# Three, not six, activation sums of the last feed-forward product kept in DRAM, and the sums of the first feed-forward matmul placed later in the program

## The chip, the cores and the metric

The kernel runs on one core of a Trainium2 chip. The metric is the device time of one execution in microseconds (us); lower is better. The engines of the core work from queues of their own and wait for each other through semaphores: PE (TensorE, matrix multiplication), ACT (ScalarE), DVE (VectorE), POOL (GpSimd) and SP (SyncE, which here only issues DMAs). An engine takes its instructions in the order of its program; an instruction that waits holds up those behind it.

## What is computed

One decoder layer on 1024 tokens of 1024 channels in float32: a pooling and attention mixer, a normalised residual, a feed-forward block, a second normalised residual, and a gated input at the end. The change lies in the feed-forward block and in what is prepared for the gate beside it:

```
h  = layer_norm(ALPHA * x + concat(pool, attn) @ w_out)      # 1024 x 1024
ff = square(relu(h @ w_ff1)) @ w_ff2                         # 1024 -> 4096 -> 1024
h  = layer_norm(ALPHA * h + ff)
gate = sigmoid(h @ w_ple_gate + b_ple_gate)                  # 1024 x 1024
out  = h + gate * (p @ w_ple)
```

## The kernel before, in words

**Number format.** Every matrix product is made of three PE passes (`mm3`, L115 to L117). Each operand is split into a high part, which ACT casts (`high`, L100), and a low part, which DVE gets by subtraction (`low`, L105); the passes are high by high, high by low and low by high. So before PE can multiply a fresh operand, ACT and then DVE must have been over it.

**Products in seven.** The feed-forward matmuls work on 2 x 2 blocks with seven block products in place of eight, so sums and differences of blocks are needed on the way. These are the DVE additions of `add` (L120).

**First feed-forward matmul.** The 4096 hidden channels are 16 pairs `p` of two 128-channel blocks; two pairs make a quad `q`. For each pair there are up to seven products, `a11, s2, s3, s1, a12, s4, a22` in this order (the first eight pairs did `a11` and `a12` earlier in the program). A product is 12 matmuls of 512 columns. The loop over `order` splits the weight operand of the product four places ahead (`AHEAD`), then multiplies the present one (`prod`), then calls `finish`, which forms the activation blocks. Split weights live in the six buffers of tag `ws` (`part`). When the second pair of a quad is done, the four blocks of activations are written to DRAM by POOL's queue (`f_dram`, L680). In this loop two extra pieces of work are placed:

- `hidden_sum(q)` (L700 on): one DVE addition of two activation blocks of the quad, in place (`v = v + ...`, 128 x 1024), and a DMA of the sum to `s_dram[q]` on POOL's queue (L702). It is wanted by the very last of the seven products of the second matmul, number 2, whose left operand is the sum of two blocks. It is done for six quads (`NQUAD - NKEEP`), each being queued in `late` and taken from it at a product `s3` of an even pair. Since it overwrites a block that is also being written to `f_dram`, it must wait until that write has ended.
- `weight_sums(k)`, for k = 0 to 3 at pairs 6 to 9: two DMAs bring rows of `w_gate` (L691, into two `ws` buffers), four DVE additions form sums of them, four DMAs put them into DRAM (`g_dram`, L697) for the gate matmul at the end. All of it stands behind product `s1` of the pair.

At the start of the last four pairs' products, four `pre` buffers of weights for the second matmul are fetched (L761), partly with a summing DMA on POOL's queue (L766).

**Second feed-forward matmul.** Seven products (`SEQUENCE` = 1, 5, 4, 3, 7, 6, 2) over eight quads each (`QORDER` = 6, 7, 0, 1, 2, 3, 4, 5) make 56 units. A unit is 24 matmuls. Quads 6 and 7 are still in SBUF; the others are read back once into `hidden` (six buffers of tag `c`) and stay there. While unit u is multiplied, `prepare(u + 1)` splits its operands, the activations into `w` (two buffers) and the weights into `right` (tile `x7`, shown as `x`). A left operand that is a sum is added on DVE into a `st` buffer (two of them); in product 2, for quads 0 to 5, `fetch_sum` instead loads it from `s_dram` into such a buffer by SP's queue (L776).

During product 2, SP's queue also carries the weights (L761), the write and the four reads of a transposition through DRAM for each normalised block (`flip`, L429 and L431), and the loads of the gate's weights (`gate_load`, L109). Each gate load needs a `ws` buffer and is split by ACT and DVE into a `c` buffer; `c` in the rows below is such a split gate weight, `w` and `x` are the two operands of the next unit.

A scheduler that simulates the program sets the final order on each engine, so instructions move by some places beyond what the code says.

Of the kernel before, what the change touches and what calls it, by code (L numbers as in the profile page):

```python
# [7 lines left out]
F32 = mybir.dt.float32  # L8
# [4 lines left out]
P = 128  # L13
D = 1024
S = 1024
HALF = 512
# [4 lines left out]
NQUAD = NPAIR // 2  # L21
# [27 lines left out]
NKEEP = 2  # L49
# [10 lines left out]
}  # L60
BLOCK = {"a11": 0, "a12": 1, "a21": 2, "a22": 3}
NPRE = 8
PLAIN = 4
HALVES = (slice(0, HALF), slice(HALF, D))
NLAST = NPAIR - 4
# [4 lines left out]
def layer(ctx, tc, xT, x, pT, w_in, w_pool, pscale, sinks, w_out, ln1, w1, w2, ln2, w_ple, w_gate, bgate, bias, rcount, out):  # L70
# [48 lines left out]
    def add(o, a, b, op=ALU.add):  # L119
        nc.vector.tensor_tensor(out=o, in0=a, in1=b, op=op)  # L120
# [14 lines left out]

    h_dram = [tc.dram_tile([P, D], F32, name=f"hd{n}") for n in range(NT)]
    t_dram = [tc.dram_tile([P, 4, 2 * P], F32, name=f"td{n}") for n in range(2 * NT)]
    s_dram = [tc.dram_tile([P, 2, HALF], F32, name=f"sd{q}") for q in range(NQUAD - NKEEP)]
    g_dram = {t: [tc.dram_tile([P, 2, HALF], F32, name=f"g{t}{i}") for i in range(2)] for t in ("T1", "T2", "T3", "T4")}
    f_dram = [tc.dram_tile([P, 2, 2, 2, HALF], F32, name=f"fd{q}") for q in range(NQUAD - NKEEP)]  # L140

# [531 lines left out]
    def hidden_block(p, m, n, make):  # L673
        key = (p // 2, m, n)
        if key not in FF:
            FF[key] = nat([P, 2, HALF])
        dst = FF[key][:, p % 2, :]
        make(dst)
        if p % 2 and p // 2 < NQUAD - NKEEP:
            nc.gpsimd.dma_start(out=f_dram[p // 2][:, m, n], in_=FF[key])  # L680
            if n == 1:
                made.append(key)
                if len(made) % 2 == 0:
                    late.append(lambda q=p // 2: hidden_sum(q))

    made, late, sums_a = [], [], {}

    def weight_sums(k):
        r = [part((P, 2, HALF), F32) for _ in range(2)]
        for i in range(2):  # L690
            nc.sync.dma_start(out=r[i], in_=w_gate[(4 * i + k) * P : (4 * i + k + 1) * P, :].rearrange("p (h c) -> p h c", h=2))  # L691
        add(r[0][:, 0], r[0][:, 1], r[0][:, 0], ALU.subtract)
        add(r[0][:, 1], r[1][:, 1], r[0][:, 1], ALU.subtract)
        add(r[1][:, 1], r[1][:, 1], r[0][:, 0], ALU.subtract)
        add(r[1][:, 0], r[1][:, 0], r[1][:, 1], ALU.subtract)
        for name, i, h in (("T1", 0, 0), ("T3", 0, 1), ("T2", 1, 1), ("T4", 1, 0)):
            nc.sync.dma_start(out=g_dram[name][k // 2][:, k % 2], in_=r[i][:, h])  # L697
# [73 lines left out]

    def fetch_sum(u):
        i, q = units[u]
        if i == 2 and q < NQUAD - NKEEP:
            sums_a[u] = stage([P, 2, HALF])
            nc.sync.dma_start(out=sums_a[u], in_=s_dram[q])  # L776

    ready = {}
    for i in range(len(order) + AHEAD):
        if i == order.index((NLAST, "a11")):  # L780
            begin = wide("pre", [P, 4, 2, HALF], F32)
            for u in range(4):
                fetch(u)
        if i < len(order):
            with tc.issue_after((diff[3][1] if i == AHEAD else lows[-1]).ins):
                ready[i] = w_split(source(*order[i]))
        if i < AHEAD:
            continue
        p, name = order[i - AHEAD]
        xb, where, more = STEPS[name]  # L790
        if not more:
            B[p, where] = bank()
        prod(B[p, where], ready.pop(i - AHEAD), xb, more)
        if late and p % 2 == 0 and name == "s3":
            late.pop(0)()
        if 6 <= p < 10 and name == "s1":
            weight_sums(p - 6)
        finish(p, name)
        if i - AHEAD < 4:
            with tc.issue_after(diff[3][1].ins):  # L800
                last_sum(i - AHEAD)
# [347 lines left out]
```

## Time and profile before

| what | us |
|---|---|
| runs shown | 985.11, 986.88, 988.04 |
| median of the runs shown | 986.88 |
| the profiled execution's own time | 986.92 |
| its span, first to last instruction | 985.1 |
| first feed-forward loop on PE, about | 320 to 569 |
| second feed-forward matmul on PE, about | 569 to 878 |
| product 2, its last eighth, about | 834 to 878 |

Times in the text count from the start of the span. In a timeline row, the first number is the start, the second the duration, then engine, source line, operation, written tile <- read tiles; in brackets is the idle time of the engine before the row and what ended it. A matmul row's duration is longer than the distance to the next start, because matmuls overlap; it is the distance of starts that tells whether PE is held up. In the chain of waits a row is start, duration, and what was done or waited for. "SPq" rows are the issue of a DMA by SP's queue.

### The profile page before, as it was taken

Reading aid. Unit: us, or ns where it says so; the run is one execution under the profiler, and the core shown is the slowest. Engines: PE = TensorE matmul, PEld = TensorE weight load, DVE = VectorE, ACT = ScalarE, POOL = GpSimd, SP = SyncE. Lnnn points to the kernel's source line nnn. Section 1 sums busy time; section 2 is a strip of 40 time slices with the busy share of each in tenths; the row PEclk is TensorE's granted clock in tenths of the full one; section 3 lists DMA queues with packets and bytes.
Section 4 is the critical chain, followed back from the end, with each engine's and each line's share of the span. In section 5 each row is a group of like instructions: output and inputs, shape, how many; then the busy total and the mean of one; then the engine's idle time right before and its main releaser. Section 6 shows DMA issues by size and latency. Waiting matters only on the chain.

```text
span 985.1 us, 12301 instructions
## 1 busy us (share of the span) xinstructions
PE 975.0 (99%) x4474; PEld 808.3 (82%) x4474; DVE 750.0 (76%) x1188; ACT 470.9 (48%) x749; POOL 110.0 (11%) x148
## 2 busy tenths in 40 slices
PE   9999999999999999999999999999999999999998
PEld 7888887888888888888888888888888888878887
DVE  5798888895869877667557766887647699599985
ACT  5676666543576434433444433433433344454341
POOL 0013552020010000111000000100011110001000
PEclk9999999999999999999999999999999999999999
DMA  6512142623162644897364793676798867962741
GB/s 220 182 65 86 44 150 86 203 92 112 65 214 86 211 153 149 305 297 264 114 258 172 291 319 137 157 249 193 196 225 186 227 158 231 287 200 92 240 150 54
DMA packets 52125, 175.28 MB, mean 178 GB/s; under 512 B 6112, under 2 KB 11360, under 8 KB 49248
## 3 DMA queue, kind: packets, MB, share of 16 engines
q1 hardware_dynamic: 41776, 140.02, 42.2%
q0 software_dynamic: 8704, 29.89, 12.2%
q10 hardware_dynamic: 1584, 4.59, 1.2%
q8 instruction: 35, 0.57, 0.2%
q14 instruction: 26, 0.21, 0.1%
HBM read 140.39 MB, written 34.08 MB: 177 GB/s over the span
## 4 chain that ended last, share of the span: by engine, by line
PE 84%; DVE 6%; DMA 5%; issue 3%; ACT 1%; POOL 0%; SPq 0%; DVEq 0%; ACTq 0%; POOLq 0%
PE f L117 18%; PE f L116 18%; PE f L115 18%; PE mm L115 8%; PE mm L116 8%; PE mm L117 8%; DMA ws<-in_w_gate 3%; DMA fd<-n 1%; PE pt L321 1%; DVE w L105 1%; PE s L298 1%; PE s L297 1%; DMA td<-n 1%; DVE x L105 1%; DVE st L120 1%
## 5 line engine op out<-in xcount | busy, mean ns | idle before, releaser
L116 PE MATMUL f<-x,w 128*128 128x512 f32 x448 | 174.3, 390 | 0.9 <-DVE x L105 0.9
L117 PE MATMUL f<-x,w 128*128 128x512 f32 x448 | 173.9, 389 | 0.0
L115 PE MATMUL f<-c,ws 128*128 128x512 f32 (+1 forms) x420 | 162.6, 387 | 0.0
L116 PE MATMUL f<-c,ws 128*128 128x512 f32 (+1 forms) x420 | 162.5, 387 | 0.0
L117 PE MATMUL f<-c,ws 128*128 128x512 f32 (+1 forms) x420 | 161.6, 388 | 0.5 <-DVE ws L105 0.5
L115 PE MATMUL f<-x,w 128*128 128x512 f32 x448 | 147.3, 390 | 0.9 <-ACT x L100 0.9
L100 ACT CAST w<-st 128x1024 fp32r<-128x1024 f32 (+2 forms) x66 | 65.6, 998 | 100.0 <-issue 58.0
L105 DVE TENSOR_TENSOR w<-st,w 128x1024 fp32r<-128x1024 f32 (+2 forms) x66 | 77.5, 1176 | 46.7 <-ACT w L100 46.5
L116 PEld LDWEIGHTS f<-x,w 128*128 128x128 f32 x448 | 84.1, 188 | 20.0 <-DVE x L105 2.6
L115 PEld LDWEIGHTS f<-x,w 128*128 128x128 f32 x448 | 83.9, 188 | 19.2 <-ACT x L100 1.8
L117 PEld LDWEIGHTS f<-x,w 128*128 128x128 f32 x448 | 84.1, 188 | 17.2
L117 PEld LDWEIGHTS f<-c,ws 128*128 128x128 f32 x420 | 78.8, 188 | 17.7 <-DVE ws L105 1.7
L116 PEld LDWEIGHTS f<-c,ws 128*128 128x128 f32 x420 | 78.9, 188 | 16.2
L115 PEld LDWEIGHTS f<-c,ws 128*128 128x128 f32 x420 | 78.9, 188 | 16.0
L105 DVE TENSOR_TENSOR x<-ws,x 128x1024 fp32r<-128x1024 f32 x54 | 65.7, 1217 | 0.1
L100 ACT CAST ws<-st 128x512 fp32r<-128x512 f32 x48 | 29.8, 621 | 65.7 <-DVE st L120 34.6
L100 ACT CAST x<-ws 128x1024 fp32r<-128x1024 f32 x54 | 56.6, 1049 | 5.2 <-PE f L117 3.5
L115 PE MATMUL mm<-c,w 128*128 128x512 f32 x144 | 56.1, 394 | 0.5 <-ACT w L100 0.5
L117 PE MATMUL mm<-c,w 128*128 128x512 f32 x144 | 56.5, 393 | 0.0
L116 PE MATMUL mm<-c,w 128*128 128x512 f32 x144 | 56.3, 392 | 0.0
L105 DVE TENSOR_TENSOR ws<-w,ws 128x512 fp32r<-128x512 f32 x60 | 41.0, 688 | 20.2 <-ACT ws L100 19.8
L100 ACT CAST ws<-w 128x512 fp32r<-128x512 f32 x60 | 36.8, 621 | 39.9 <-PE f L117 21.9
(234 smaller groups left out, 1884.2 us busy)
## 6 DMA issues: line engine op xcount, KB each, us to landing
ws<-in_w SPq DMA_DIRECT2D x70, 512.0 KB, 3.8
w<-in_w SPq DMA_DIRECT2D x16, 1024.0 KB, 5.1
c<-fd SPq DMA_DIRECT2D x6, 2048.0 KB, 9.1
fd<-n POOLq DMA_DIRECT2D x20, 512.0 KB, 4.4
ws<-in_w POOLq DMA_DIRECT2D x20, 512.0 KB, 7.7
st<-in_w_in SPq DMA_DIRECT2D x17, 512.0 KB, 3.3
ws<-in_w_gate SPq DMA_DIRECT2D x16, 512.0 KB, 6.2
w<-in_w SPq DMA_DIRECT2D x10, 512.0 KB, 3.8
```

The source lines that it names most:

```text
L100: nc.scalar.copy(out=dst, in_=src)
L105: return eng.tensor_tensor(out=dst, in0=src, in1=hi.bitcast(F32), op=ALU.subtract)
L115: nc.tensor.matmul(o, ah, bh, start=first, stop=False, skip_group_check=more)
L116: nc.tensor.matmul(o, ah, bl, start=False, stop=False, skip_group_check=more)
L117: nc.tensor.matmul(o, al, bh, start=False, stop=last, skip_group_check=more)
L120: nc.vector.tensor_tensor(out=o, in0=a, in1=b, op=op)
L297: nc.tensor.matmul(s[:, i, dst], ql, kt[:, 0, g, kk : kk + kn], start=True, stop=False)
L298: nc.tensor.matmul(s[:, i, dst], ql, kt[:, 1, g, kk : kk + kn], start=False, stop=True)
L321: nc.tensor.transpose(pt[:, i, :], e[:, i, kb * P : (kb + 1) * P], ident)
```

## The change

`hidden_sum` is now made for the first three quads only (`NSUM = 3`). For quads 3, 4 and 5 the sum goes through `prepare` as all other sums do: one DVE addition of the two blocks in `hidden`, into a `st` buffer, in place of the load. Those sums that remain are taken from `late` at product `s4`, not `s3`. The two parts of `weight_sums` are parted: the loads stand behind `s2`, one product earlier than before for these two DMAs, and the additions and stores behind `a22`, the last product of the pair.

```diff
+NSUM = 3
...
-    s_dram = [tc.dram_tile([P, 2, HALF], F32, name=f"sd{q}") for q in range(NQUAD - NKEEP)]
+    s_dram = [tc.dram_tile([P, 2, HALF], F32, name=f"sd{q}") for q in range(NSUM)]
...
-                if len(made) % 2 == 0:
+                if len(made) % 2 == 0 and p // 2 < NSUM:
                     late.append(lambda q=p // 2: hidden_sum(q))
...
-    def weight_sums(k):
+    def weight_rows(k):
         r = [part((P, 2, HALF), F32) for _ in range(2)]
         for i in range(2):
             nc.sync.dma_start(out=r[i], in_=w_gate[...])
+        return r
+
+    def weight_sums(k, r):
         add(r[0][:, 0], r[0][:, 1], r[0][:, 0], ALU.subtract)
...
-        if i == 2 and q < NQUAD - NKEEP:
+        if i == 2 and q < NSUM:
             sums_a[u] = stage([P, 2, HALF])
             nc.sync.dma_start(out=sums_a[u], in_=s_dram[q])
...
-        if late and p % 2 == 0 and name == "s3":
+        if late and p % 2 == 0 and name == "s4":
             late.pop(0)()
-        if 6 <= p < 10 and name == "s1":
-            weight_sums(p - 6)
+        if 6 <= p < 10 and name == "s2":
+            rows = weight_rows(p - 6)
+        if 6 <= p < 10 and name == "a22":
+            weight_sums(p - 6, rows)
```

The line numbers of the changed kernel are one higher at L105 and L120 and up to six higher further down; tile numbers differ too. Where it moves instructions:

**DVE in the first matmul, at pair 9's first weights** (`w_3900` before and `w_3899` now are that pair's raw weights, `ws` a split or, in `ws_3875`, a row pair of `w_gate`, `n` an activation block). Before:

```order
L120 TENSOR_TENSOR n_3930<-t_3898,f_3905 128x512
L105 TENSOR_TENSOR ws_3902<-w_3900,ws_3902 128x512
L120 TENSOR_TENSOR st_3934<-w_3900 128x512
L120 TENSOR_TENSOR st_3934<-st_3934,w_3900 128x512
L120 TENSOR_TENSOR n_3709<-n_3709,n_3690 128x1024
L105 TENSOR_TENSOR ws_3937<-st_3934,ws_3937 128x512
```

Now:

```order
L121 TENSOR_TENSOR n_3917<-t_3897,f_3904 128x512
L106 TENSOR_TENSOR ws_3901<-w_3899,ws_3901 128x512
L121 TENSOR_TENSOR st_3921<-w_3899 128x512
L121 TENSOR_TENSOR st_3921<-st_3921,w_3899 128x512
L106 TENSOR_TENSOR ws_3924<-st_3921,ws_3924 128x512
L121 TENSOR_TENSOR w_3899<-w_3899 128x512
L121 TENSOR_TENSOR ws_3875<-ws_3875 128x512
```

The in-place sum of quad 3, `n_3709`, is gone from ahead of the split of pair 9's second operand, and the first addition of the third group of gate rows comes three rows behind that place.

**DVE in the first matmul, at the fourth group of gate rows** (`ws_4066` and `ws_4067` before, `ws_4023` and `ws_4024` now; `t`, `n` are activation sums). Before:

```order
L105 TENSOR_TENSOR ws_4085<-st_4082,ws_4085 128x512
L120 TENSOR_TENSOR w_4048<-w_4048 128x512
L120 TENSOR_TENSOR ws_4066<-ws_4066 128x512
L120 TENSOR_TENSOR ws_4066<-ws_4067,ws_4066 128x512
L120 TENSOR_TENSOR ws_4067<-ws_4067,ws_4066 128x512
L120 TENSOR_TENSOR ws_4067<-ws_4067 128x512
L120 TENSOR_TENSOR n_3971<-t_4028,f_4053 128x512
```

Now:

```order
L121 TENSOR_TENSOR ws_4023<-ws_4023 128x512
L121 TENSOR_TENSOR t_4045<-t_4027,f_4032 128x512
L106 TENSOR_TENSOR ws_4029<-w_3899,ws_4029 128x512
L121 TENSOR_TENSOR n_3917<-t_4045,f_4052 128x512
L121 TENSOR_TENSOR ws_4023<-ws_4024,ws_4023 128x512
L106 TENSOR_TENSOR ws_4049<-w_4047,ws_4049 128x512
L121 TENSOR_TENSOR st_4069<-w_4047 128x512
L121 TENSOR_TENSOR ws_4024<-ws_4024,ws_4023 128x512
L121 TENSOR_TENSOR st_4069<-st_4069,w_4047 128x512
L121 TENSOR_TENSOR ws_4024<-ws_4024 128x512
L106 TENSOR_TENSOR ws_4072<-st_4069,ws_4072 128x512
```

The four additions stood in one block and are now spread among the splits and activation sums; the last of them stands before the split that it used to follow.

**DVE in product 2** (`c` a split gate weight, `w` and `x` the operands of the next unit, `st` the sum of two activation blocks). Before:

```order
L105 TENSOR_TENSOR x_711_4952<-ws_6689,x_711_4952 128x1024
L105 TENSOR_TENSOR c_6815<-ws_6816,c_6815 128x1024
L105 TENSOR_TENSOR w_6828<-st_6778,w_6828 128x1024
L105 TENSOR_TENSOR x_711_4952<-ws_6728,x_711_4952 128x1024
L105 TENSOR_TENSOR c_6815<-ws_6820,c_6815 128x1024
L105 TENSOR_TENSOR w_6870<-st_6826,w_6870 128x1024
L105 TENSOR_TENSOR x_711_4952<-ws_6776,x_711_4952 128x1024
L105 TENSOR_TENSOR c_6857<-ws_6858,c_6857 128x1024
```

Now:

```order
L106 TENSOR_TENSOR x_711_4943<-ws_6680,x_711_4943 128x1024
L121 TENSOR_TENSOR st_6857<-c_5060 128x1024
L106 TENSOR_TENSOR c_6806<-ws_6807,c_6806 128x1024
L106 TENSOR_TENSOR w_6817<-st_6769,w_6817 128x1024
L106 TENSOR_TENSOR x_711_4943<-ws_6719,x_711_4943 128x1024
L121 TENSOR_TENSOR st_6920<-c_5096 128x1024
L106 TENSOR_TENSOR c_6806<-ws_6811,c_6806 128x1024
L106 TENSOR_TENSOR w_6859<-st_6857,w_6859 128x1024
L106 TENSOR_TENSOR x_711_4943<-ws_6767,x_711_4943 128x1024
L121 TENSOR_TENSOR st_6962<-c_5137 128x1024
L106 TENSOR_TENSOR c_6846<-ws_6847,c_6846 128x1024
```

Three additions come in, each behind an `x` and ahead of the `c` that follows it; the rest keeps its order. SP's queue at the same place before:

```order
L109 DMA ws_6816<-in_w_gate 128x2x512
L776 DMA st_6826<-sd_102 128x1024
L431 DMA n_7127<-td_93 32x4x256 x2
L109 DMA ws_6820<-in_w_gate 128x2x512
L431 DMA n_7127<-td_93 32x4x256 x2
L761 DMA ws_6824<-in_w 128x1024
L776 DMA st_6868<-sd_103 128x1024
L109 DMA ws_6858<-in_w_gate 128x2x512
L109 DMA ws_6862<-in_w_gate 128x2x512
L776 DMA st_6931<-sd_104 128x1024
L761 DMA ws_6866<-in_w 128x1024
```

Now:

```order
L110 DMA ws_6807<-in_w_gate 128x2x512
L432 DMA n_7118<-td_93 32x4x256 x2
L110 DMA ws_6811<-in_w_gate 128x2x512
L432 DMA n_7118<-td_93 32x4x256 x2
L765 DMA ws_6815<-in_w 128x1024
L110 DMA ws_6847<-in_w_gate 128x2x512
L110 DMA ws_6851<-in_w_gate 128x2x512
L765 DMA ws_6855<-in_w 128x1024
```

The three loads of sums have gone from between the gate loads; nothing else has changed places here.

## The prediction

> **What bounds the kernel now.** The page's first part comes first:
>
> ```profile
> PE 975.0 (99%) x4474; PEld 808.3 (82%) x4474; DVE 750.0 (76%) x1188; ACT 470.9 (48%) x749; POOL 110.0 (11%) x148
> ```
>
> PE is busy for 975.0 of 985.1 us and the change takes no matmul away. So all that can be won is time in which PE is held up. A busy PE may still be held up a little, so next comes the table of 20-us stretches (busy PE time and, in brackets, matmul records):
>
> ```profile
> 480.00:500.00 20.00, 20.00 (x90) 1.00 0.53 184
> 420.00:440.00 20.00, 19.80 (x88) 1.00 1.03 336
> 460.00:480.00 20.00, 19.73 (x87) 1.00 0.34 125
> 860.00:880.00 20.00, 18.21 (x76) 1.00 0.71 228
> ```
>
> From 320 to 960 nearly every stretch is like the first of these, at 89 or 90 records. The ones that are clearly short lie at 420 to 440, 460 to 480 and 860 to 880: just where the change works. Then the PE timeline, to size the holes:
>
> ```profile
> 855.06 0.39 PE L116 MATMUL f<-x,w 128*128 128x512 f32 x1
> 857.33 0.39 PE L117 MATMUL f<-x,w 128*128 128x512 f32 x1
> ...
> 437.43 0.39 PE L116 MATMUL f<-c,ws 128*128 128x512 f32 x1
> 438.01 0.50 PE L117 MATMUL f<-c,ws 128*128 128x512 f32 x1 [0.20 <-DVE ws L105]
> ...
> 460.18 0.39 PE L116 MATMUL f<-c,ws 128*128 128x512 f32 x1
> 460.84 0.50 PE L117 MATMUL f<-c,ws 128*128 128x512 f32 x1 [0.27 <-DVE ws L105]
> ...
> 862.88 0.39 PE L117 MATMUL f<-x,w 128*128 128x512 f32 x1
> 865.66 0.50 PE L116 MATMUL f<-x,w 128*128 128x512 f32 x1 [0.44 <-DVE x L105]
> ...
> 870.11 0.39 PE L117 MATMUL f<-x,w 128*128 128x512 f32 x1
> 872.31 0.50 PE L116 MATMUL f<-x,w 128*128 128x512 f32 x1 [0.42 <-DVE x L105]
> ```
>
> The first two rows are ten starts apart, so matmuls start every 0.227 us when nothing holds them. At 437 the next start comes after 0.58 us, 0.35 late; at 460 after 0.66, 0.43 late. From 862.88 to 865.66 there are five starts, worth 1.14 us, and it took 2.78: 1.64 late. From 870.11 to 872.31, five again, 2.20: 1.06 late. The first matmul after a hole is recorded 0.11 longer (0.50, not 0.39), and the start after it is late by about that. With it the four holes are **0.46, 0.54, 1.75 and 1.17 us, together 3.9**. That is the most that the change can take away there.
>
> **The first matmul, DVE's two long waits.** Both small holes are waits for a low part that DVE made late:
>
> ```profile
> 436.13 1.23 DVE L120 TENSOR_TENSOR n<-n,n 128x1024 f32<-128x1024 f32 x1 [5.53 <-DMA fd<-n]
> 437.27 0.68 DVE L105 TENSOR_TENSOR ws<-st,ws 128x512 fp32r<-128x512 f32 x1
> ...
> 424.17 11.94 DMA fd<-n
> ...
> 455.36 0.69 DVE L120 TENSOR_TENSOR ws<-ws 128x512 f32<-128x512 f32 x1 [2.24 <-DMA ws<-in_w_gate]
> 456.84 1.42 DVE L120 TENSOR_TENSOR ws<-ws,ws 128x512 f32<-128x512 f32 x2 [0.79 <-DMA ws<-in_w_gate]
> ...
> 449.26 7.49 DMA ws<-in_w_gate
> ```
>
> The first is the in-place sum of quad 3: it may not overwrite its block before the write to DRAM that POOL issued at 424.17 has landed, 11.94 us later, and the split that PE needs stands right behind it. In the changed order this sum does not exist (the `n<-n,n` row is gone from between the two splits), so DVE's 5.53 us of standing still go, and with them the hole of **0.46 us**. What is late next there: the raw weights are in SBUF and the split is ready to run, so nothing that I see.
>
> The second is the fourth group of gate rows: its load is issued at 449.26, lands 7.49 us later, and DVE, in order, waits 2.24 and 0.79 us for it. Now the loads stand behind `s2` and the additions behind `a22`, so a load has four or five products, 11 to 14 us at 12 times 0.227 us each, before it is wanted; the four additions are spread out, and splits stand between them. I take the **0.54 us** as gone too. Of what is moved with it: the two DMAs of a group come earlier on SP's queue, ahead of the next pair's raw weights and of the `pre` loads; the four additions (0.69 us each) and four stores come later, the same number as before. The price, if their cover goes, is that two of the six `ws` buffers are held longer. Then the splits run fewer places ahead, and DVE and ACT have less of a start when they are held up.
>
> How much of a start the splits have, the first wait tells: 5.53 us of it cost PE 0.46, so about 5.1 us of a wait in one block is free. The three removed sums also take 3 times 1.2 us from DVE and three stores from POOL in this loop; nothing waits on these but what is named, so I set them at nothing. Bounds for this loop: 1.0 us gained at best, the two holes; at worst one such wait comes back under another name at 1.0 us lost. I take 1.0 gained, since both rows that made the holes are gone or moved by more than they were late.
>
> **Product 2, from 843 on.** The chain of waits runs here through gate loads and DVE, and DVE's and SP's timelines show how they interlock:
>
> ```profile
> 849.34 1.22 DVE L105 TENSOR_TENSOR c<-ws,c 128x1024 fp32r<-128x1024 f32 x1 [4.72 <-ACT c L100]
> 851.62 1.22 DVE L105 TENSOR_TENSOR x<-ws,x 128x1024 fp32r<-128x1024 f32 x1
> 854.91 1.22 DVE L105 TENSOR_TENSOR c<-ws,c 128x1024 fp32r<-128x1024 f32 x1 [2.07 <-ACT c L100]
> 857.19 1.22 DVE L105 TENSOR_TENSOR x<-ws,x 128x1024 fp32r<-128x1024 f32 x1
> 860.87 2.46 DVE L105 TENSOR_TENSOR c<-ws,c 128x1024 fp32r<-128x1024 f32 x2 [2.47 <-ACT c L100]
> 864.39 1.22 DVE L105 TENSOR_TENSOR x<-ws,x 128x1024 fp32r<-128x1024 f32 x1
> ...
> 843.51 0.33 SPq L776 DMA_DIRECT2D st<-sd  x1
> 847.89 0.40 SPq L109 DMA_DIRECT2D ws<-in_w_gate  x1
> 851.73 0.34 SPq L776 DMA_DIRECT2D st<-sd  x1
> 857.30 0.60 SPq L776 DMA_DIRECT2D st<-sd  x1
> ...
> 847.89 5.90 DMA ws<-in_w_gate
> 856.16 4.84 DMA ws<-in_w_gate
> 863.37 4.28 DMA ws<-in_w_gate
> ```
>
> A gate load (`in_w_gate`) lands, ACT casts it, DVE makes its low part (`c`), and only that frees a buffer for a later load. The operands `w` and `x` of PE's next unit stand behind each `c` on DVE. So a late gate load makes `x` late (864.39 plus 1.22 is 865.61, and PE starts at 865.66).
>
> *The three added sums.* Each is a `st<-c` row, 1.22 us by this group, and starts about 1.14 us after the row before it. In the changed order they stand behind `x` and ahead of the next `c`: in DVE's idle times of 4.72, 2.07 and 2.47 us above. All three are long enough, so they cost nothing there; if the cover were gone, 3 times 1.14 is 3.4 us.
>
> *The three removed loads.* These were issued at 843.51, 851.73 and 857.30, 512 KB each, on the queue that carries the gate loads:
>
> ```profile
> st<-sd SPq DMA_DIRECT2D x5, 512.0 KB, 5.5
> ws<-in_w_gate SPq DMA_DIRECT2D x8, 512.0 KB, 4.7
> ```
>
> (issues from 835 to 875, with the median time to landing). The gate load of 847.89 had the first of them ahead of it and took 5.90; that of 863.37, with none close ahead, 4.28. Without the sums I let the former take 4.84, as the load of 856.16 did. It lands at 852.7, is cast by 853.8, and DVE, free at 853.9 after its added sum (851.62 + 1.14 + 1.14), starts `c` then and not at 854.91: 1.0 us sooner. The load that was issued at 856.16 waits for the buffer that this `c` frees, so it goes at 855.15, lands 4.84 later at 860.0, and its `c`, cast 1.1 us on, comes 1.0 sooner as well; so do `w` and `x` behind it. The next two loads wait for those `c`s, so the second hole shifts by the same 1.0. PE therefore leaves the second hole **1.0 us** sooner. That is not the sum of both holes: the chain of load, cast, `c` and buffer is shorter by 1.0 and no more.
>
> Bounds here: nothing, if the loads take as long as before (the added sums then fill idle time only). With 4.28 for every load, DVE's added sum still sets the first `c` at 853.9, but the later load goes at 855.1 and lands at 859.4: about 1.7 us gained. On the losing side the 3.4 us above, if the sums found no idle time.
>
> On latency the skill has a rule of its own. The Trainium skill, "DMA: Bandwidth & Descriptors", section "Anatomy of one DMA — SWDGE (gpsimd) path", gives for POOL's own loads about 2.0 us plus bytes over 436 GB/s, an estimate of 3.2 us for 512 KB. By that rule the loads would be sooner still, some 2.4 us gained here and 983.5 in all. The trace does not agree: its quickest row above is 4.28 and the median 4.7.
>
> *Does the time won in the first matmul last to here?* ACT tells:
>
> ```profile
> 835.78 1.06 ACT L100 CAST w<-st 128x1024 fp32r<-128x1024 f32 x1 [3.38 <-PE f L117]
> ```
>
> It waits 3.38 us for PE to free a `w` buffer, so this stretch is timed by PE, and a PE that is 1.0 us early brings it all forward by 1.0. The two terms add.
>
> **Sum.** 1.0 in the first matmul and 1.0 in product 2 make 2.0 us. The profiled execution took 986.92 us (span 985.1 and some 1.8 around it), which is the median of the runs shown (986.88) to 0.04. So 986.9 - 2.0 = **984.9 us**, a gain of 0.2%.
>
> **Rivals.**
>
> *Quicker loads.* The gate loads take 4.28 each and 1.7 us go in product 2, or the small late starts near 852, 858 and 877 close too: 986.9 - 1.0 - 1.7 = 984.2, and down to 983 if nearly all 3.9 go. For it: DMA is the last link of the chain. Against: each `c` then waits for DVE's own sum.
>
> *No change.* The gate loads take as long as before, since the reads of the transposition stay among them on the queue, and in the first matmul another wait takes the place of the two: 986.9. For it: the load of 856.16 took 4.84 though the sum behind it was issued only after it.
>
> *Slower: gate rows in the crowd.* In the first matmul, the second group of gate rows and the third are now loaded at about the time of the summing DMAs on POOL's queue. A load there is slow:
>
> ```profile
> ws<-in_w_gate SPq DMA_DIRECT2D x1, 512.0 KB, 12.5
> ```
>
> (the one issued at 408.45). If such a load is issued only just ahead of its first addition, DVE stands for 10 to 12 us in front of splits, and all above 5.1 us falls on PE: 5 to 7 us. That eats the first term and more; with a hole of 5 us for that loop in place of the two of 1.0, and 1.0 still won in product 2, it is 986.9 - 1.0 + 5 - 1.0 = 989.9, and 992 with 7. It decides itself at a DVE wait of 5.1 us. Against it: the loads now have 11 to 14 us, and the added distance is larger than the delay. The Trainium skill, "TensorE: Matmul & The Clock Gate", section "What's actually happening", says that PE's clock halves after an idle window of about 3.4 us, which would add to such a hole; no hole here is near that, and the clock column above is 1.00.
>
> *Sums that find no room.* If the loads come so soon that DVE no longer idles ahead of `c`, up to 3.4 us are added to it: 986.9 - 1.0 + 3.4 = 989.3. But then the loads are early and `c` as well, so this eats its own cause.
>
> **How the numbers follow.** Chances: the forecast 0.50, quicker loads (the page's rule among them) 0.22, no change 0.16, slower by gate rows 0.08, sums without room 0.04. The range that leaves no more than 2 in 10 out takes in the forecast, the quicker loads and no change: from 983.0 (nearly all holes gone) to 987.6 (no change, and the spread of the runs shown, 985.11 to 988.04, of which a median keeps about half). A measurement tells about 0.3%, 3.0 us, from no change: below 983.9 or above 989.9. Of the quicker loads about two thirds, and of the forecast a fifth by the spread of runs, fall below: 0.25. Above lie the gate rows and a little of the rest: 0.10. The remaining 0.65 is no difference that can be told.
>
> **What would show it.** DVE's timeline near 436 without a wait for `fd`, and near 455 with waits for `in_w_gate` under a microsecond: first term right. PE's rows there at 0.227 apart. In product 2, the sums in idle time, `c` at about 854 and 861 (less the shift), and holes near 863 and 870 of some 2 us together in place of 2.9. Wrong if a new hole of PE stands elsewhere between 400 and 470, if the gate loads land as late as before, or if DVE has no idle time left ahead of `c`.

## The result and the profile after

The changed kernel takes **985.17 us** (median of 15 runs, 983.37 to 986.31) against 986.88 for the kernel before (15 runs, 985.11 to 989.76). The ratio is 0.998, with a 95% interval of 0.9971 to 0.9989: a gain of 1.1 to 2.9 us, 2.0 by the ratio and 1.7 by the medians. The forecast was 984.9. The profiled execution took 984.32 (span 982.5), so between the two profiles lie 2.6 us.

The page's first line and the table of 20-us stretches of the changed kernel, which answer to those of before:

```profile
PE 974.1 (99%) x4474; PEld 808.6 (82%) x4474; DVE 750.4 (76%) x1188; ACT 471.1 (48%) x749; POOL 108.6 (11%) x145
```

```profile
420.00:440.00 20.00, 20.00 (x90) 16.56 (x89) 11.45 (x18) 8.20 (x14) 2.02 (x3) 1.00 1.04 308
460.00:480.00 20.00, 20.00 (x90) 16.57 (x89) 13.97 (x22) 10.50 (x19) 0.53 (x1) 1.00 0.27 96
860.00:880.00 20.00, 19.50 (x84) 15.19 (x83) 18.96 (x23) 11.05 (x11) 0.00 (x0) 1.00 0.64 206
```

The two stretches of the first matmul are full now, with 90 matmuls like any other (88 and 87 before). The last one has 84 where it had 76. One hole of more than 0.3 us is left in it, in the PE timeline of the changed kernel:

```profile
867.38 0.39 PE L118 MATMUL f<-x,w 128*128 128x512 f32 x1
867.83 1.20 PE L116 MATMUL f<-x,w 128*128 128x512 f32 x4
869.46 0.50 PE L117 MATMUL f<-x,w 128*128 128x512 f32 x1 [0.43 <-DVE x L106]
```

From 867.38 to 869.46 there are five starts, worth 1.14 us, and it took 2.08. With the 0.11 of the next start that is 1.05 us, where the second hole of before was 1.17. The first one, 1.75 near 863, is gone altogether.

DVE's timeline of the changed kernel at the place of the first hole of before (in brackets the wait ahead of a row, and what ended it):

```profile
433.63 0.69 DVE L121 TENSOR_TENSOR ws<-ws 128x512 f32<-128x512 f32 x1 [1.70 <-DMA ws<-in_w_gate]
434.72 1.28 DVE L121 TENSOR_TENSOR n<-t,f 128x512 f32<-128x512 f32 x2 [0.39 <-DMA pre<-in_w]
438.26 0.69 DVE L121 TENSOR_TENSOR ws<-ws,ws 128x512 f32<-128x512 f32 x1 [2.26 <-DMA ws<-in_w_gate]
438.87 0.69 DVE L106 TENSOR_TENSOR ws<-w,ws 128x512 fp32r<-128x512 f32 x1
```

No row waits for `fd` any more. The parted gate rows still make DVE wait three times (1.70 and 2.26 us for the third group, and 2.21 us at 446.71 for the fourth), and PE stays full.

DVE in product 2 of the changed kernel:

```profile
843.97 1.22 DVE L121 TENSOR_TENSOR st<-c 128x1024 f32<-128x1024 f32 x1
848.36 1.23 DVE L106 TENSOR_TENSOR c<-ws,c 128x1024 fp32r<-128x1024 f32 x1 [3.17 <-ACT c L101]
...
851.77 1.22 DVE L121 TENSOR_TENSOR st<-c 128x1024 f32<-128x1024 f32 x1
853.37 1.23 DVE L106 TENSOR_TENSOR c<-ws,c 128x1024 fp32r<-128x1024 f32 x1 [0.38 <-ACT c L101]
...
856.78 1.22 DVE L121 TENSOR_TENSOR st<-c 128x1024 f32<-128x1024 f32 x1
857.91 2.36 DVE L106 TENSOR_TENSOR c<-ws,c 128x1024 fp32r<-128x1024 f32 x2
```

The three added sums (`st<-c`) lie in what used to be idle time ahead of `c`: 4.72, 2.07 and 2.47 us of waiting have become 3.17, 0.38 and none. The third leaves no idle time: the `c` behind it had its cast at about 857.2 and starts at 857.91. It is the first of a pair, and the chain below goes through the second, whose cast ends only at 859.0. The `c` of 854.91 now starts at 853.37 and that of 860.87 at 857.91.

The chain of waits of the changed kernel shows what times the hole that is left (start, duration, what was done or waited for):

```profile
839.06 6.94 DMA td<-n
...
846.96 5.30 DMA ws<-in_w_gate
...
853.37 1.24 DVE c L106
854.62 3.31 DMA ws<-in_w_gate
...
860.30 4.51 DMA ws<-in_w_gate
...
868.19 1.23 DVE x L106
```

And the ends of the same chain before:

```profile
839.80 7.14 DMA td<-n
...
871.03 1.23 DVE x L105
```

The links are the same as before; the way from the transposition's write to `x` took 31.23 us (871.03 less 839.80) and takes 29.13. Of these 2.1 us, 1.9 lie in the three gate loads: 5.30 + 3.31 + 4.51 = 13.12 us, against 5.90 + 4.84 + 4.28 = 15.02.

### The profile page after: what moved, and what is told of

It is laid out like the page before. It is cut to its first block, busy times and chain, and to the rows that moved or that the text cites. A ratio compares the mean times of both kernels' runs of the same rounds, so it can differ in the third digit from the quotient of the medians.

```text
span 982.5 us, 12277 instructions
## 1 busy us (share of the span) xinstructions
PE 974.1 (99%) x4474; PEld 808.6 (82%) x4474; DVE 750.4 (76%) x1188; ACT 471.1 (48%) x749; POOL 108.6 (11%) x145
## 4 chain that ended last, share of the span: by engine, by line
PE 94%; DMA 3%; DVE 2%; issue 1%; ACT 1%; SPq 0%; DVEq 0%
PE f L118 21%; PE f L117 21%; PE f L116 21%; PE mm L117 8%; PE mm L118 8%; PE mm L116 8%; DMA ws<-in_w_gate 1%; PE pt L322 1%; PE s L299 1%; PE s L298 1%; DMA td<-n 1%; PE av L328 1%; PE av L327 1%; DMA n<-in_xT 1%; DVE c L106 0%
```

## Experiments

One table first, for all kernels: the median time, its ratio to the kernel before with a 95% interval (those without one ran once), and, from their tables of stretches, the matmuls of 420 to 480 and of 834 to 880 and the data rate in the latter. A matmul missing is 0.227 us lost. The experiments were run in three groups, each on another chip with the kernel before beside it, and a ratio goes by that: 986.03 us beside e1 to e4, 986.79 beside e5, e9, e10 and e11, 986.63 beside e7 and e13 to e15. So kernels of different groups are compared by their ratios.

| kernel | us | ratio | 420:480 | 834:880 | GB/s |
|---|---|---|---|---|---|
| before | 986.88 | | 261 | 189 | 261 |
| changed | 985.17 | 0.998 [0.9971, 0.9989] | 265 | 198 | 234 |
| e15, changed again | 984.84 | 0.9983 [0.9974, 0.9993] | 267 | 200 | 236 |
| e1, three sums only | 984.57 | 0.998 [0.997, 0.999] | 263 | 202 | 238 |
| e2, places only | 992.71 | 1.0059 [1.0045, 1.0073] | 237 | 191 | 271 |
| e3, sums at `s4` only | 988.29 | | 256 | 190 | 265 |
| e4, rows parted only | 994.44 | | 239 | 192 | 268 |
| e11, e2 without quad 3 | 985.54 | 0.9985 [0.9976, 0.9994] | 266 | 189 | 249 |
| e13, product 2 only | 985.99 | 0.9991 [0.9983, 1.0] | 263 | 197 | 230 |
| e14, first matmul only | 986.13 | 0.9994 [0.9985, 1.0003] | 266 | 190 | 261 |
| e5, bytes put back | 985.94 | 0.9989 [0.998, 0.9999] | 267 | 189 | 262 |
| e9, six tiles | 985.20 | | 266 | 198 | 232 |
| e7, no sums | 985.90 | 0.9989 [0.998, 0.9998] | 267 | 188 | 194 |
| e10, gate loads later | 988.21 | 1.0012 [1.0002, 1.0021] | 266 | 201 | 218 |

### The change taken apart: e1 to e4

*e1, three sums only*: the places of the sums and of the gate rows stay as before.

```diff
-                if len(made) % 2 == 0:
+                if len(made) % 2 == 0 and p // 2 < NSUM:
...
-        if i == 2 and q < NQUAD - NKEEP:
+        if i == 2 and q < NSUM:
```

> Only the number of sums is changed (three, not six); they stay at s3 and the gate rows and their additions stay together at s1. Theory A (each hole has its own part of the change as its cause): the hole near 437 (0.46 us) is gone, the hole near 460 (0.54 us) is there as before, and the holes of product 2 shrink as in the changed kernel, from about 2.9 us (near 863 and 870, and 0.3 more in two small ones) to about 1.2. PE ends about 2.4 us sooner than in the kernel before. Theory B (product 2 gains only because the first loop runs ahead by itself): product 2 keeps more than 2 us of holes, and PE ends less than 1 us sooner.

984.57 us, ratio 0.998 [0.997, 0.999]: all of the gain, with none of the moves. The hole at 437 is gone. The one at 460 is there, 0.60 us, with the undivided gate rows in front of it; in product 2 the holes are 0.40 near 869 and 0.27 near 875.

*e2, places only*: the changed kernel with six sums.

```diff
-NSUM = 3
+NSUM = 6
```

> Six sums as before, but at s4, and the gate rows loaded behind s2 and added behind a22. Theory A: the hole near 460 is gone (0.54 us), product 2 keeps its holes of about 2.9 to 3.2 us, the hole near 437 stays if quad 3's in-place sum still waits for its block's write, so PE ends 0.5 to 1.0 us sooner. Theory B: product 2's holes shrink with the early start of 0.5 to 1 us, and PE ends more than 1.5 us sooner.

992.71 us, ratio 1.0059 [1.0045, 1.0073]: **the moves alone make the kernel 6 us slower**, which neither theory foresaw. The profiled execution was the slowest of e2's five, 994.75 us. e2's DVE timeline, its chain of waits, and its PE timeline show where:

```profile
433.75 0.68 DVE L121 TENSOR_TENSOR ws<-ws 128x512 f32<-128x512 f32 x1
443.21 1.23 DVE L121 TENSOR_TENSOR n<-n,n 128x1024 f32<-128x1024 f32 x1 [8.78 <-DMA fd<-n]
```

```profile
427.83 0.88 POOL pre L770
...
431.69 11.49 DMA fd<-n
```

```profile
442.76 0.39 PE L117 MATMUL f<-c,ws 128*128 128x512 f32 x1
446.88 0.80 PE L118 MATMUL f<-c,ws 128*128 128x512 f32 x1 [3.74 <-DVE ws L106]
447.48 0.63 PE L116 MATMUL f<-c,ws 128*128 128x512 f32 x1
447.90 0.63 PE L117 MATMUL f<-c,ws 128*128 128x512 f32 x1
```

It is the wait of before's first hole, only longer. POOL issues quad 3's write to DRAM at 431.69, not at 424.17: it stands behind the last summing DMA (`pre`), which goes at 427.83 here and at 419.03 before. The write lands at 443.18, and the in-place sum has held DVE for 8.78 us. PE stands still for 3.9 us. Behind it the matmuls start 0.43 us apart, not 0.227, until 452.60, which costs 2.9 us more. The table of stretches of e2 has the granted clock in its third column from the right:

```profile
446.00:449.00 3.00, 2.12 (x5) 1.73 (x6) 3.00 (x6) 1.91 (x4) 0.00 (x0) 0.51 0.62 249
449.00:452.00 3.00, 3.00 (x8) 2.32 (x8) 3.00 (x6) 0.62 (x1) 0.00 (x0) 0.50 0.81 277
```

The Trainium skill, "TensorE: Matmul & The Clock Gate", section "What's actually happening", says that the clock falls to half after an idle window of about 3.4 us. The trace agrees: PE idled for 3.74 us and was granted 0.51 and 0.50.

*e3, sums at `s4` only* (six sums, rows undivided), and *e4, rows parted only* (six sums, taken at `s3`), one run each:

```diff
-        if late and p % 2 == 0 and name == "s3":
+        if late and p % 2 == 0 and name == "s4":
```

> Only the place of the six sums is changed (s4, not s3). Theory A: quad 3's sum still has to wait for the write of its block, which landed 11.94 us after its issue at 424.17 and so about 2.7 us (one product) beyond the place s4; the wait of DVE shrinks from 5.53 to about 3 us, below the 5.1 us that are free, and the hole near 437 goes or falls below 0.2 us. The holes near 460 and in product 2 stay. Rival: the wait stays at 5 us since the write is also made later, and the hole stays at 0.4 to 0.5 us.

988.29 us, inside the 984.80 to 990.06 of the kernel before beside it. The wait for quad 3's write is 6.58 us, and PE's hole at 437 is 2.1 us, not 0.46. But the edit moved nothing: on every engine, e3's trace has the operations and tiles of the kernel before in the same order (buffer numbers left out). So e3 is that order executed once more, and the hole varies that much from one execution to another.

```diff
-        if 6 <= p < 10 and name == "s1":
-            weight_sums(p - 6)
+        if 6 <= p < 10 and name == "s2":
+            rows = weight_rows(p - 6)
+        if 6 <= p < 10 and name == "a22":
+            weight_sums(p - 6, rows)
```

> Six sums at s3 as before; only the gate rows are loaded behind s2 and added behind a22. Theory A: the hole near 460 is gone, product 2 keeps 2.9 to 3.2 us, and the hole near 437 stays at about 0.46 us. Rival: by taking the gate rows' loads out of the crowd of summing DMAs, the write of quad 3's block lands sooner as well and the hole near 437 goes too.

994.44 us. The wait is 9.36 us, the hole 4.5, with half clock behind it; again neither expectation held. Here too the place of the sums moved nothing: the orders of e4's trace are those of e2's, and its time lies within e2's 990.41 to 994.75. So it is the parting of the rows that makes the moves harmful. Before and e3, e2 and e4 are four executions of two orders, and they give DVE's wait and PE's hole: 5.53 and 0.46, 6.58 and 2.1, 8.78 and 3.9, 9.36 and 4.5. The 5.1 us of free wait that the prediction took from the first pair gives 1.5, 3.7 and 4.3 for the other three. It is a figure for this place alone: at 460, waits of 2.24 and 0.79 us stood ahead of a hole of 0.54 in the kernel before.

### Quad 3 alone: e11

e2 with five sums: that of quad 3 is made in product 2.

```diff
-NSUM = 6
+HELD = (0, 1, 2, 4, 5)
...
-                if len(made) % 2 == 0 and p // 2 < NSUM:
+                if len(made) % 2 == 0 and p // 2 in HELD:
...
-        if i == 2 and q < NSUM:
+        if i == 2 and q in HELD:
```

> As the kernel with six sums and parted rows that was 0.6% slower than before, but the sum of quad 3 alone is not made early; it is added in product 2 (five sums in DRAM). Theory A (the hole of 3.9 us near 443 is the in-place sum of quad 3 that waits for its own block's write to DRAM, and the half clock behind it follows from that hole): no wait for fd on DVE there, no hole near 443, matmuls at 0.227 us apart, and some 6 us less than that kernel's 992.7: 985.5 to 987. Rival B (parting the rows makes the hole by itself, through the buffers or the queue): the hole stays with another wait in front of it, above 990. The hole near 410 stays if it is due to the six tiles or to the other sums.

985.54 us, ratio 0.9985: theory A holds. e11's DVE timeline where e2 stood for 8.78 us, and its stretch of PE:

```profile
435.22 1.29 DVE L121 TENSOR_TENSOR n<-t,f 128x512 f32<-128x512 f32 x2 [2.18 <-PE f L118]
436.42 0.68 DVE L121 TENSOR_TENSOR ws<-ws,ws 128x512 f32<-128x512 f32 x1
```

```profile
440.00:460.00 20.00, 20.00 (x90) 16.57 (x89) 14.65 (x25) 9.13 (x16) 2.16 (x4) 1.00 0.75 271
```

DVE waits here for PE, not PE for DVE, and 90 matmuls are done where e2 had 59, with its hole and the half clock behind it. Quad 3's write lands late here as well (issued at 430.68, 11.82 us), as it does in the changed kernel (429.16, 12.60 us): nobody waits for it. e11 also spares product 2 one load, but it does 189 matmuls from 834 to 880 as before, so its gain over e2 is not from there. In e2's profile the hole and the half clock cost 6.8 us, and without this one in-place addition, whose block was still on its way to DRAM, both are gone. (e2's other hole, of 1.4 us near 410, is 0.3 in e11; that part is not explained, see e9.)

### The two terms apart: e13, e14, e5, e15

*e13, product 2 only*: the kernel before, with the three loads replaced by additions, and all six sums still made.

```diff
-        if i == 2 and q < NQUAD - NKEEP:
+        if i == 2 and q < 3:
```

> The kernel before with one part of the change: product 2 adds the sums of quads 3, 4 and 5 on DVE and no longer loads them. The six sums are still made and stored in the first matmul, three of them for nobody, and all places there are as before. Theory A (the gain is that of the three loads taken out of product 2, and nearly all of it): the holes of PE at 437 and 460 stay at about 0.5 each, the two of product 2 fall from 2.9 together to about 1, and the time is 1.5 to 2.2 us under before, ratio 0.9978 to 0.9985. Rival B (product 2 gains only because PE and the transposition arrive earlier from the first matmul): the holes of product 2 stay above 2, ratio 0.999 to 1.

Its chain has the same links, with loads of 5.22, 4.15 and 3.83 us (13.20 together, 15.02 before):

```profile
848.03 5.22 DMA ws<-in_w_gate
...
855.62 4.15 DMA ws<-in_w_gate
...
862.13 3.83 DMA ws<-in_w_gate
```

The holes of product 2 fall from 3.4 us (1.75, 1.17 and two small ones of 0.24 and 0.27) to 1.7, and those at 437 and 460 stay, 0.46 and 0.31. The mechanism is theory A's; in the runs the gain is 0.6 us by the medians, ratio 0.9991 [0.9983, 1.0], less than the 1.5 to 2.2 expected.

*e14, first matmul only*: e1, and the bytes of the three loads put back as copies from DRAM to DRAM that nobody reads, at the old places on SP's queue. *e5, bytes put back*: the same on the changed kernel.

```diff
+        elif i == 2 and q < NQUAD - NKEEP:
+            with tc.issue_after((gate_loads[0] if q == 3 else fetched[-2] if q == 4 else gate_loads[3]).ins):
+                nc.sync.dma_start(out=x_dram[q - NSUM], in_=s_dram[q - NSUM])
```

> The kernel with three sums (its places as before the change), with the bytes of the three removed loads put back as three 512-KB copies from DRAM to DRAM on SP's queue at their old places, into a tile that nobody reads. Theory A (these bytes are the price that the tail paid): the hole at 437 is gone (0.4 won), gate loads take 4.5 us or more, the holes of product 2 are back at 2 to 3 us together, ratio 0.9989 to 0.9997. Rival B (the removed loads cost through the st buffer they held, not through their bytes): the time is that of three sums alone, ratio 0.998.

> The changed kernel with the bytes of the three removed loads put back: three 512-KB copies from DRAM to DRAM on SP's queue, at the places of the removed loads, into a tile that nobody reads. DVE's order is that of the changed kernel, with its three added sums. Theory A (the gate loads land sooner because 1.5 MB less share the DMA engines with them): the gate loads of product 2 take 4.5 to 6 us again, c comes 1 us or more later than in the changed kernel, the second hole of PE near 867 grows from 1.05 to 2 to 3 us, and the time is 986.0 to 987.0. Rival B (it was not the bytes but the removed loads' hold on a buffer and on the order of SP's queue): the gate loads take 3.3 to 4.5 as in the changed kernel, and the time is its 985.2 within 0.4.

e14: 986.13 us, 0.9994 [0.9985, 1.0003]. e5: 985.94 us, 0.9989 [0.998, 0.9999]. In both, the first matmul is full (266 and 267 matmuls from 420 to 480) and product 2 is as it was before: 190 and 189 matmuls, holes of 3.2 and 3.5 us. No copy holds a buffer that anything waits for, and DVE's order in e5 is that of the changed kernel. e14 also has no hole at 460, though its rows are undivided and its DVE order is e1's; nor has e10, with waits for the rows of 2.23 and 0.62 us. So that hole comes and goes between executions. e5's chain and its DMA table (issues of 840 to 868, with the median time to landing):

```profile
848.90 5.11 DMA ws<-in_w_gate
...
856.37 4.55 DMA ws<-in_w_gate
```

```profile
ws<-in_w_gate SPq DMA_DIRECT2D x7, 512.0 KB, 4.5
xd<-sd SPq DMA_DIRECT2D x3, 512.0 KB, 5.8
```

The load that took 3.31 takes 4.55 here, but a single load tells little: in e15, the changed kernel again, it took 4.38. The chain's three gate loads together do tell. They took 12.6 to 13.5 us in the profiles without the removed loads (the changed kernel, e1, e9, e13, e15) and 13.9 to 15.1 in those with them or with copies (before, e2, e3, e5, e14). So theory A holds in the traces: **what product 2 paid for was the three loads' transfers on a busy queue**, not their buffers. Whether it is their bytes or their number, these runs do not part. In the runs e5 comes out just below what was expected (986.0 to 987.0, measured 985.94); its interval and that of the changed kernel overlap, so the traces carry this more than the times do.

*e15, changed again*: the changed kernel beside these parts.

> The changed kernel itself, run beside the parts of it on the same chip. Theory A (the terms of the first matmul and of product 2 don't add, since a chain of loads times the last hole of product 2): the same as product 2's part alone within 0.5 us. Rival B (they add): 0.8 to 1.0 us less than product 2's part alone.

984.84 us, 1.15 us less than e13, where theory A said at most 0.5 and rival B 0.8 to 1.0. That speaks for rival B and against theory A, which e1 had suggested; but the two intervals overlap, so the times alone don't exclude theory A. By the ratios, e13 gains 0.9 us and e14 0.6, together 1.5; the whole gains 1.7. In matmuls of the two stretches, e13 wins 2 and 8, e14 5 and 1, the whole 4 to 6 and 9 to 11. **The terms add**, as near as this can tell. Only the half microsecond at 460 isn't seen at the end: e1 keeps that hole and is no later, since its product 2 loses less (202 matmuls; 198, 200 and 198 in three profiles of the changed program). One profile of e1 doesn't tell whether that is its loads' luck or the chain at work, and the times can't tell 0.5 us.

### What else was tried: e9, e7, e10

*e9, six tiles.* e2 and e4 have another hole, of 1.4 and 1.8 us near 410, ahead of anything that differs in the order of any engine from the changed kernel. The test reserves six tiles for sums and uses three.

```diff
-    s_dram = [... for q in range(NSUM)]
+    s_dram = [... for q in range(NQUAD - NKEEP)]
```

> The changed kernel with six tiles for the sums reserved in DRAM, of which three are used, as before. No instruction is added, removed or moved; only addresses in DRAM shift. Theory A (the hole of PE near 410, 1.4 to 1.8 us, that both kernels with six sums and parted rows showed and that the changed kernel doesn't, comes from where the tiles lie): the hole is there. Rival B (it comes from elsewhere, the order on the queues or chance): no hole near 410, and a time of 985.2 within 0.8.

985.20 us, and no hole near 410: not the tiles. e15 shows 0.3 us there and e11 0.2. Its cause stays open.

*e7, no sums*: all six are added in product 2.

```diff
-NSUM = 3
+NSUM = 0
```

> The changed kernel with no sum at all through DRAM: all six are added on DVE in product 2, and none is made in the first matmul. Theory A (any sum taken out of the loads helps, since DVE finds the time): 984.5 to 985.2, no new hole. Rival B (an added sum is only free where DVE idles ahead of c; the first three fall into 820 to 842, where DVE stands behind its work): PE gets new holes there of up to 1.1 us per sum, 986 to 988.5 in all.

985.90 us, ratio 0.9989 [0.998, 0.9998]. The data rate is the lowest of all, 194 GB/s, and yet 188 matmuls is the lowest count. DVE's timeline and PE's:

```profile
838.12 1.23 DVE L106 TENSOR_TENSOR w<-st,w 128x1024 fp32r<-128x1024 f32 x1
839.25 1.23 DVE L121 TENSOR_TENSOR pre<-pre,ws 128x1024 f32<-128x1024 f32 x1
840.38 1.24 DVE L106 TENSOR_TENSOR x<-ws,x 128x1024 fp32r<-128x1024 f32 x1
841.52 1.23 DVE L121 TENSOR_TENSOR st<-c 128x1024 f32<-128x1024 f32 x1
```

```profile
841.67 0.50 PE L117 MATMUL f<-x,w 128*128 128x512 f32 x1 [0.79 <-DVE x L106]
```

Around 840 DVE works without a gap, so the sums for quads 0 to 2 push `x` back and PE waits for it (a hole of 1.06). Two further holes, of 1.4 at 852 and about as much from 869 on, have ACT's cast or DVE's low part of `x` in front of them. Rival B's mechanism holds for the hole near 840 (its time, 986 to 988.5, was a little too high), and with it the prediction's rival of sums without room: true of the first three sums, not of the last three.

*e10, gate loads later*: e1, with the last four gate loads placed so that DVE makes `w` and `x` of the last unit ahead of their `c`.

```diff
-            if k >= 2:
+            if k in (2, 3):
                 gate_load(k - 2)
+            if k >= 6:
+                with tc.issue_after(lows[-1].ins), tc.issue_after(casts[-1].ins):
+                    for j in (2 * k - 10, 2 * k - 9):
+                        gate_load(j)
```

> Three sums only (places of the sums and rows as before the change), and the last four gate loads of product 2 placed so that DVE makes the low parts of the last unit's operands w and x ahead of those loads' low parts. Theory A (the last hole of PE in product 2 is timed by the chain of gate loads, whose low part c stands ahead of x on DVE): x no longer waits for c, the holes near 864 and 868 close (some 0.7 to 1.2 us gained against the kernel with three sums only, 984.6), so 983.4 to 983.9. Rival B (the gate loads then land later, PE ends sooner but the gate matmul after it waits for its operand): PE's holes close, but the time comes back behind product 2: 984.6 within 0.4, or above.

988.21 us, ratio 1.0012 [1.0002, 1.0021]. The hole near 868 closes (201 matmuls), so `x` did wait behind `c`. But the time comes back, and more, as rival B had it. e10's chain and PE timeline:

```profile
880.32 1.90 DVE c L106 x2
882.22 3.80 DMA ws<-in_pT
```

```profile
883.69 0.39 PE L118 MATMUL f<-c,ws 128*128 128x512 f32 x1
887.14 0.50 PE L116 MATMUL f<-c,c 128*128 128x512 f32 x1 [3.06 <-ACT c L101]
...
888.85 0.63 PE L116 MATMUL f<-c,ws 128*128 128x512 f32 x1
889.28 0.63 PE L117 MATMUL f<-c,ws 128*128 128x512 f32 x1
```

The later `c` frees its buffer later, the load of the next matmul's operand goes at 882.22 (874.04 in the changed kernel), and PE waits 3.06 us for its cast, with half clock behind: 5.0 us in all. The chain of gate loads is the right place for the last hole, but this order only moves it.

## Why the prediction was right, step by step

**The ceiling.** 3.9 us of holes were named as all there was to win; 2.6 were won in the profile, and what is left of the four is 1.05. Right.

**Hole 437 (0.46).** Right in cause: with quad 3's sum gone there is no wait for `fd`, and no hole in the changed kernel, e1, e7 or e14. e11 shows that this one sum is enough. The size is that of one execution; e3, with the same orders, had 2.1 there. That about 5.1 us of a DVE wait in one block is free foretold the holes of e2, e3 and e4 within 0.6, but it doesn't hold at 460.

**Hole 460 (0.54).** The hole did go, but the reason given for it is not shown. The gate rows had not the 11 to 14 us that I gave them: the three loads that DVE waited for were issued 12.3, 7.8 and 4.9 us ahead of their additions, and the waits are 1.70, 2.26 and 2.21 us, not under a microsecond as the sign asked. And of the kernels that keep the rows undivided, e1 has a hole of 0.60 there and e14 and e10 have none, so the parting need not be what closed it. At the end e1 is as fast without it. What the parting does by itself the prediction missed: it saw two `ws` buffers held longer and 1.0 us lost at worst. POOL's write of quad 3, behind the summing DMAs, goes at 431.69 in e2 and 432.61 in e4, 424.17 before, and this costs them 6 us or more. The changed kernel issues it at 429.16 and doesn't pay, since its other half takes the waiting sum away. I looked at the two DMAs of a group on SP's queue, not at what the moved order did on POOL's.

**The added sums (nothing).** Right for the chain: they fall into 4.72, 2.07 and 2.47 us of idle time. The third uses up all of its own, because `c` came sooner, and holds the next `c` back by some 0.7 us; that `c` was not the one on the chain. e7 shows the price where there is no idle time.

**The removed loads (1.0, bounds 0 to 1.7).** The mechanism was right, the size too small: from the transposition's write to `x` the chain took 31.23 us in the profile of before and 28.8 to 29.1 in those of the changed kernel, e9, e13 and e15. (In e3, with the orders of before, it took 29.84, so part of this is the one execution.) The mis-sized step is the loads' time. I took 4.84 us for the first two and left the third at 4.28, 13.96 together. They took 5.30, 3.31 and 4.51, 13.12 together. The second, which I left as it was, gave 1.5 of the 1.9 us in this profile, though only 0.5 of 1.5 in e15. My reason for leaving it was that its sum was issued only after it. I overlooked what was still in flight ahead of it: in the kernel before, the sum issued at 851.73 took 5.5 us and the gate load of 852.86 behind it 6.9, so neither had landed at 856.16. e5 and e14 put all three back at once and don't tell which of them weighs.

The gain went beyond my upper bound because I took the quickest gate row of before, 4.28, as the floor. The page of that same profile has other loads of this size on SP's queue with a quicker median:

```profile
st<-in_w_in SPq DMA_DIRECT2D x17, 512.0 KB, 3.3
```

The Trainium skill's rule ("DMA: Bandwidth & Descriptors", section "Anatomy of one DMA — SWDGE (gpsimd) path"), an estimate of 3.2 us for 512 KB, comes near that row and near the quickest of the changed kernel's three, 3.31. The other two took 5.30 and 4.51 with more in flight on the queue. Two sums of the prediction also come out otherwise from the same rows: with 4.28 for each load the second lands 1.6 us sooner, not 1.7, and with 3.2 for each the third would land 3.7 sooner, not 2.4, more than the two holes hold.

**The terms add.** Right within what can be told (e13, e14, e15), save for the half microsecond at 460, which comes and goes.

**Sum.** 2.0 us forecast; 1.7 by the medians, 2.0 by the ratio, 2.6 in the profiles. The profile of before lay on its median, that of the changed kernel 0.85 us below its own. So the forecast of the time came out close also because a term that was 1.1 too small met medians that show less than the profiles do.

**The rivals.** Quicker loads: true of one load of three in this profile, and the chain as a whole passed its 1.7 us. No change: refuted by the interval. Slower by gate rows in the crowd: the price (5 to 7 us) and the point of decision (a wait of 5.1 us) came true in e2 and e4, but by another DMA, a write on POOL's queue and not the gate rows; in the changed kernel the rows' waits are 1.70, 2.26 and 2.21. Sums without room: not here, but in e7.

## What to carry to other kernels

An in-place operation behind an outstanding write is a stall that waits for its moment: it costs little until something delays the write, and then it holds up all that stands behind it on its engine. When work is moved, look at every queue that it shares with others, also at those whose own instructions are not touched. A transfer replaced by an addition pays where a chain of loads shares its queue and the engine idles, and costs where the engine doesn't; so count the idle time at each place by itself, three of the six sums here and not all. And look whether an edit moved anything at all: taking the sums at `s4` did not, and one order executed twice showed holes of 0.46 and 2.1 us at one place.

## What the runs showed that was not expected

**Half clock after a hole near 3 us.** In e10 PE idled for 3.06 us, ran 1.3 us with starts 0.23 us apart, and only then fell to 0.43 us, from 888.43 to 891.41 (granted clock 0.50). In e4, after 4.32 us, the fall came 0.9 us behind the restart; in e2, after 3.74 us, it was slow at once. Beyond the hole itself that cost 1.7 us in e10, 1.7 in e4 and 2.9 in e2. The Trainium skill, "TensorE: Matmul & The Clock Gate", section "What's actually happening", says that the window runs freely, so that the moment of the change depends on where in it the first matmul falls. The three traces agree in that the moment varies; but the 3.06 us of e10 are less than the idle window of about 3.4 us, and the clock fell all the same.

**A start that varies.** In the profiles of these kernels, PE's hundredth matmul comes between 0.27 us earlier and 1.16 us later than in that of the kernel before, though the orders there are the same, and the shift then stays until the kernels differ. That is as much as each term of this change, and may be part of why 1 us is plain in a trace and hardly seen in a median of a dozen runs.
